# Attention logits of both heads of a pair on the two halves of the array, and a gate mask without the query's own sum

## The chip, the cores and the metric

The kernel runs on one core of one Trainium2 chip. The metric is device time in microseconds; the kernel before took 1919.86 us (median of three runs, 1917.96 to 1921.83). The core has a matrix engine (PE, with its weight loads shown apart as PEld), a vector engine (DVE), a scalar engine (ACT), a third elementwise engine (POOL) and DMA queues, which are fed by SP. Each engine runs its own instructions in a fixed order and waits on semaphores for the others.

## The reference, cut to what matters

Two transformer blocks run one after the other on 512 tokens of width 1024. The first block has two layers. Each layer has four kinds of attention with four heads each, then an output projection per kind and a feed-forward part. The second block (dilated attention, pooling, gates) is not part of the change.

```python
for l in range(2):                       # first block
    proj = rms_norm(x, norm1[l]) @ w_in[l]
    o_a = causal attention, head width 96 (latent)
    o_b = sliding window of 128 keys, with a sink logit
    o_c = causal attention over the 128 best keys of each query (indexer, top-k)
    o_d = causal attention with a forget gate:
          s = q.k/8 + (cum[t] - cum[s]);  s = where(s_pos <= t_pos, s, -inf);  softmax(s) @ v
    x = x + concat(o_a, o_b, o_c, o_d) @ w_out[l]
    x = x + square(relu(rms_norm(x, norm2[l]) @ w_up[l])) @ w_down[l]
```

In the gated attention (`o_d`) the term cum[t] of the query is the same for all its keys, so that the softmax does not depend on it.

## The kernel before, in words

All products are made from numbers split into a high and a low part, so that one product is three matmuls: high by high, high by low, low by high (`mm3`, L159 to L161 in the profile). Four blocks of 128 tokens are handled one by one.

A layer's attention part goes, in the order of the program text, through the letters of `ORDER = "LI123AZVPDCBadcb"`: latent inputs (L), indexer (I), index scores and top-k of blocks 1 to 3 (1, 2, 3), latent attention of two pairs of heads (A, Z), gated values (V) and keys (P), gated attention (D), selected attention with its own projections (C), sliding window with its own projections (B), and the four output projections (a, d, c, b). A scheduler then places the instructions of each engine. It favours what comes first in the text and moves later work into places where an engine would otherwise wait; the order is fixed when the kernel is built. The top-k rounds (L574 maximum of 8, L575 replace, L576 the mask) have a low priority and fill DVE. So projections of a later letter fill PE between the steps of an earlier attention.

Attention works on a pair of heads (`mixed_pair`). For each head, `softmax` makes four blocks of logits (one for 128 queries each, over 128 to 512 keys; for the window 128 or 256). A block is three matmuls into a PSUM bank of the tag "sc" (two banks). Then DVE adds the mask and takes the row maximum in one instruction (L335), with the sums written to a tile `p` in SBUF. ACT takes the exponentials of the head's four blocks (L345) after the maxima of all four, and scales them (L355) after the reciprocal. PE transposes the blocks of `p` (L378), ACT and DVE split the transposes into `pt`, and PE multiplies them with the values (L309, L310, L312, tile `pv`). There were two `p` tiles. The heads of C, B and D are 64 wide: the q and k of the first head of a pair lie in partitions 0 to 63 of the tile `seg`, those of the second in 64 to 127. The latent heads are 96 wide. The projections write to PSUM banks of the tag "acc" (two banks), as do the output projections; the banks are free again when ACT and DVE have read them.

For the gated attention, `forgetting` loads the negated sums of the keys for one head, spread over all partitions, into the tile `nrow` (one buffer, a DMA from DRAM), and per block DVE builds a mask from `nrow`, the query's own sum and the causal mask (L811, 128x128 to 128x512) before the block's L335.

In the second block, `pair_attention` has logits of 64-wide heads too (L1174), and there the three matmuls of both heads are written alternately in the program text.

Of the kernel before, what the change touches and what calls it, by code (L numbers as in the profile page):

```python
# [11 lines left out]
F32 = mybir.dt.float32  # L12
F32R = mybir.dt.float32r
AF = mybir.ActivationFunctionType
ALU = mybir.AluOpType
# [3 lines left out]
P = 128  # L19
S = 512  # L20
# [6 lines left out]
TAKEN = -3.0e38  # L27
EPS = 1e-6
TOPK = 128
SEGS, MIXES, PBUFS, PTS, VS = 4, 5, 2, 2, 4  # L30
QKS, V2S, PB2, B2S, GATES, PT2 = 6, 3, 2, 7, 4, 3
AHEAD, RAWS, HIS, TMPS, HALVES = 2, 2, 4, 3, 4
FIRST, KZS = 3, 2
# [24 lines left out]
class Kern:  # L58
# [43 lines left out]
        return self.tmp.tile([P, D], F32, tag="tmp", name=self.name("tmp"), bufs=TMPS)  # L102

    def half(self):
        return self.tmp.tile([P, S], F32, tag="t2", name=self.name("t2"), bufs=HALVES)

    def stat(self, cols=16):
        return self.small.tile([P, 16], F32, tag="st", name=self.name("st"), bufs=11)[:, :cols]
# [203 lines left out]
            mm(out, both, th[0], start=False, stop=True)  # L312


    def softmax(self, hd):


        nc = self.nc
        spans = hd["spans"] = hd["spans"]() if callable(hd["spans"]) else hd["spans"]
        offs, tot = [], 0  # L320
        for k0, n, _ in spans:
            offs.append(tot)
            tot += n
        pb = self.att.tile([P, 1280], F32, tag="p", name=self.name("p"), bufs=PBUFS)
        hd["p"], hd["at"] = pb, offs
        mx, sm, nm, rc = (self.astat() for _ in range(4))
        for i, (k0, n, mask) in enumerate(spans):
            sc = self.psum("sc")[:, :n]
            tok = slice(i * P, (i + 1) * P)
            self.mm3(  # L330
                sc, tuple(a[:, tok] for a in hd["q"]), tuple(a[:, k0 : k0 + n] for a in hd["k"]), True, True
            )
            if callable(mask):
                mask = mask(i, n)
            nc.vector.tensor_tensor_reduce(  # L335
                out=pb[:, offs[i] : offs[i] + n], in0=sc, in1=mask, scale=1.0, scalar=TAKEN,
                op0=ALU.add, op1=ALU.max, accum_out=mx[:, i : i + 1],
            )
        if hd.get("sink") is not None:
            nc.vector.tensor_scalar(nm, mx, hd["sink"], -1.0, ALU.max, ALU.mult)  # L340
        else:
            nc.vector.tensor_scalar(nm, mx, -hd["scale"], None, ALU.mult)
        for i, (k0, n, _) in enumerate(spans):
            s = pb[:, offs[i] : offs[i] + n]
            nc.scalar.activation(  # L345
                s, s, AF.Exp, bias=nm[:, i : i + 1], scale=hd["scale"], accum_out=sm[:, i : i + 1]
            )
        if hd.get("sink") is not None:
            es = self.astat()
            nc.scalar.activation(es, nm, AF.Exp, bias=hd["sink"])  # L350
            nc.vector.tensor_tensor(sm, sm, es, ALU.add)
        nc.vector.reciprocal(rc, sm)
        for i, (k0, n, _) in enumerate(spans):
            s = pb[:, offs[i] : offs[i] + n]
            nc.scalar.activation(s, s, AF.Copy, scale=rc[:, i : i + 1])  # L355
# [4 lines left out]
    def mixed_pair(self, heads, v, order):  # L360

        nc = self.nc
        m = self.mix()
        total = sum(len(g) for g in order)
        for x, hd in enumerate(heads):
            self.softmax(hd)
            spans = hd["spans"]
            pv = self.psum("pv")
            nmm = 0
            for group in order:  # L370
                pt = self.psum("tp")
                at, cols = 0, []
                for j in group:
                    who = [i for i, (k0, n, _) in enumerate(spans) if k0 <= j * P < k0 + n]
                    cols.append((j, at, who))
                    for i in who:
                        src = hd["at"][i] + j * P - spans[i][0]
                        nc.tensor.transpose(pt[:, at : at + P], hd["p"][:, src : src + P], self.ident)  # L378
                        at += P
                th = self.new_pt()  # L380
                self.split(th[:, 0, :at], th[:, 1, :at], pt[:, :at])
                for j, a, who in cols:
                    w = len(who) * P
# [94 lines left out]
    def consts_first(self):  # L478
        nc, c, t = self.nc, self.fc, self.t

        def load(name, shape, src):
            o = c.tile(shape, F32, tag=name, name=name)
            nc.sync.dma_start(o, src)
            return o

        self.rope64 = load("rope64", [P, NB, 128], t["c_rope64"].rearrange("(b p) c -> p b c", p=P))
        self.rope32 = load("rope32", [P, NB, 64], t["c_rope32"].rearrange("(b p) c -> p b c", p=P))
        self.causal = load("causal", [P, S], t["c_causal"])
        self.swa = load("swa", [P, 256], t["c_swa"])
        self.tri = load("tri", [P, P], t["c_tri"])  # L490
        self.full_spans = [(0, (i + 1) * P, self.causal[:, S - (i + 1) * P :]) for i in range(NB)]
        self.ones = c.tile([P, P], F32, tag="ones", name="ones")
        nc.vector.memset(self.ones, 1.0)

    def indexer(self, l, hT):

        nc = self.nc
        chunks = self.weights(3)
        kst = self.att.tile([P, S], F32R, tag="nrow", name=self.name("kst"), bufs=1)
        acc = self.att.tile([P, 256 + 384 + 512], F32, tag="dsa", name=self.name("dsa"), bufs=1)  # L500
        self.dsa = [(self.causal[:, 384:512], P)]
        offs = (None, 0, 256, 640)
# [5 lines left out]
        def rotate(b):  # L508
            pj = self.token_proj(hT, chunks, b, I_N)
            if b:  # L510
                r = self.att.tile([P, 320], F32, tag="ir", name=self.name("ir"), bufs=3)[:, :I_N]
                nc.scalar.copy(r[:, 288:296], pj[:, 288:296])
                self.idx.append(r)
            else:
                r = self.half()[:, :I_N]
            h = slice(0 if b else 8, 9)
            rv = r[:, 0:288].rearrange("p (a c) -> p a c", a=9)
            self.rope(rv[:, h], pj[:, 0:288].rearrange("p (a c) -> p a c", a=9)[:, h], self.rope32, b)
            return rv
# [212 lines left out]
    def window(self, l, hT):  # L732
        nc, t = self.nc, self.t
        sink = self.att.tile([P, 4], F32, tag="sink", name=self.name("sink"), bufs=1)
        nc.sync.dma_start(sink, t["swa_sinks"][l].partition_broadcast(P))
        sg = self.seg()
        vs = [self.new_v() for _ in range(2)]

        def values(b, src):
            for g in range(2):  # L740
                self.put_v(vs[g], b, src[:, g * 64 : g * 64 + 64].unsqueeze(1).to_broadcast([P, 2, 64]))

        self.roped(hT, self.weights(2), sg, 0)
        self.roped(hT, self.weights(2), sg, 2, values)
        spans = [(max(0, i - 1) * P, P if i == 0 else 2 * P, self.swa[:, 128:] if i == 0 else self.swa)
                 for i in range(NB)]
        return self.two_pairs(
            sg, vs, BAND, spans=spans, scale=0.125, sink=lambda h: sink[:, h : h + 1]
        )
# [47 lines left out]
    def forgetting(self):  # L797
# [2 lines left out]
        sg = self.gated_seg  # L800

        def spans(hh):
            nrow = self.att.tile([P, S], F32, tag="nrow", name=self.name("nrow"), bufs=1)
            nc.sync.dma_start(
                nrow.rearrange("p (b c) -> p b c", b=NB),
                neg.rearrange("(b h) c -> h b c", h=4)[hh].partition_broadcast(P),
            )

            def bias(i, m):
                o = self.att.tile([P, S], F32, tag="bias", name=self.name("bias"), bufs=2)[:, :m]  # L810
                nc.vector.scalar_tensor_tensor(  # L811
                    o, nrow[:, :m], cum[:, i, hh : hh + 1], self.causal[:, S - m :], ALU.add, ALU.add
                )
                return o

            return [(0, (i + 1) * P, bias) for i in range(NB)]

        return self.two_pairs(sg, vs, FULL, spans=lambda h: lambda: spans(h), scale=1.0)

    def selected(self, l, hT):  # L820
# [5 lines left out]
        for b in range(NB):  # L826
            pj = self.token_proj(hT, ch, b, 256)
            for n in range(2):
                self.put_v(vs[n], b, pj[:, n * P : (n + 1) * P].rearrange("p (h c) -> p h c", c=64))
        return self.two_pairs(sg, vs, FULL, spans=[(0, n, a) for a, n in self.dsa], scale=0.125)  # L830

    def first_tiles(self, hT, block, count):

# [262 lines left out]
    def pair_inputs(self, hp, hT):  # L1096
# [12 lines left out]
        for g, which in HEADS2:  # L1109
# [12 lines left out]
            if which < 2:  # L1122
# [1 line left out]
                self.split(nat(o[:, 0]), nat(o[:, 1]), perm(pj), 0.125 if which == 0 else None)  # L1124
                qk[g, which] = o
                continue
            vT = self.half()
            nc.scalar.copy(nat(vT), perm(pj))
            v = self.new_v()
            pt = self.psum("tq")  # L1130
# [357 lines left out]
```

## Time and profile before

| | |
|---|---|
| median of three runs | 1919.86 us |
| the profiled execution | 1920.97 us, its span 1918.9 us |
| attention of layer 0, gated heads and C's projections beside them | 137 to 200.3 us |
| C, B and the output projections of layer 0 | 200.3 to 312 us |
| the same two stretches in layer 1 | 804 to 873 us, 873 to 985 us |
| PE busy over the span | 95% |
| DVE, ACT, POOL busy over the span | 62%, 44%, 29% |

The matmul rows of the profile start at the true times, but their lengths overlap: how long one occupies PE is read from the start of one to the start of the next. DVE rows overlap a little too.

### The profile page before, as it was taken

The page shows a single profiled execution, that of the slowest core. Times are in us where ns is not written, and L with a number is a line of the kernel's source. Part 1 is how long each engine was busy: PE and PEld are TensorE (multiplying, and loading weights), DVE is VectorE, ACT ScalarE, POOL GpSimd, SP SyncE. Part 2 cuts the span into 40 slices and gives each one's busy share as a digit, 9 for nine tenths or more (in the row PEclk, how much of TensorE's full clock was granted, in tenths as well). Part 3 has the DMA queues.
Part 4 walks back from the last instruction along what each step waited for, and adds up shares of the span by engine and source line. Part 5 has one row for each costly group of instructions (what it writes and reads, how often), then busy time and mean ns, then how long its engine had stood idle before and what let it go on. Part 6 is the DMA issues. An engine that isn't in the chain of part 4 may idle for free.

```text
span 1918.9 us, 25696 instructions
## 1 busy us (share of the span) xinstructions
PE 1825.1 (95%) x9414; PEld 1524.4 (79%) x9414; DVE 1184.9 (62%) x2381; ACT 852.7 (44%) x1842; POOL 565.8 (29%) x396
## 2 busy tenths in 40 slices
PE   7899998999999998999989999999798999999898
PEld 7778877888877887888778888888776787777677
DVE  6899666555545378996774443344728644559675
ACT  5656765332323256567653233233434344534223
POOL 1334331111101113343311111111245443433454
PEclk9899999999999998999999999999899999999999
DMA  5232112444465322221133333333332332322242
GB/s 160 59 83 61 45 49 80 141 144 143 134 185 156 95 66 59 81 64 45 45 99 99 99 90 98 99 88 99 114 86 59 89 100 67 88 61 78 66 148 99
DMA packets 220651, 178.51 MB, mean 93 GB/s; under 512 B 14734, under 2 KB 191278, under 8 KB 220526
## 3 DMA queue, kind: packets, MB, share of 16 engines
q1 hardware_dynamic: 220526, 176.88, 31.3%
q8 instruction: 74, 1.21, 0.3%
q14 instruction: 51, 0.42, 0.1%
HBM read 172.50 MB, written 8.03 MB: 94 GB/s over the span
## 4 chain that ended last, share of the span: by engine, by line
PE 76%; DVE 13%; DMA 5%; ACT 2%; issue 2%; POOL 1%; SPq 0%; DVEq 0%; ACTq 0%; POOLq 0%
PE acc L159 19%; PE acc L160 18%; PE acc L161 18%; PE sc L159 5%; PE sc L160 4%; PE sc L161 4%; DMA raw<-in_w_in_dram 2%; PE tp L378 2%; PE pv L310 1%; DVE p L1235 1%; DVE b L1077 1%; PE pv L309 1%; ACT whi L142 1%; DVE dsa L554 1%; DMA raw<-in_w_down_dram 1%
## 5 line engine op out<-in xcount | busy, mean ns | idle before, releaser
L142 ACT ACTIVATE whi<-raw 128x1024 fp32r<-128x1024 f32 (+6 forms) x288 | 289.2, 1005 | 621.8 <-PE acc L160 243.5
L159 PE MATMUL acc<-hTh,whi 128*128 128x512 f32 (+1 forms) x1128 | 438.0, 389 | 11.4 <-DVE kz L167 4.7
L160 PE MATMUL acc<-hTl,whi 128*128 128x512 f32 (+1 forms) x1128 | 434.6, 386 | 0.9 <-DVE hTl L167 0.9
L161 PE MATMUL acc<-hTh,wlo 128*128 128x512 f32 (+1 forms) x1128 | 434.1, 385 | 0.0
L143 POOL TENSOR_TENSOR wlo<-raw,whi 128x1024 fp32r<-128x1024 f32 (+4 forms) x143 | 312.7, 2191 | 375.8 <-ACT whi L142 354.1
L143 DVE TENSOR_TENSOR wlo<-raw,whi 128x1024 fp32r<-128x1024 f32 (+2 forms) x145 | 177.3, 1224 | 199.4 <-ACT whi L142 199.3
L871 POOL TENSOR_TENSOR tmp<-tmp 128x512 f32<-128x512 f32 x64 | 104.8, 1639 | 609.8 <-ACT tmp L869 609.8
L159 PEld LDWEIGHTS acc<-hTh,whi 128*128 128x128 f32 x1128 | 215.1, 191 | 57.6 <-issue 7.1
L160 PEld LDWEIGHTS acc<-hTl,whi 128*128 128x128 f32 x1128 | 215.0, 191 | 41.6 <-DVE hTl L167 2.4
L161 PEld LDWEIGHTS acc<-hTh,wlo 128*128 128x128 f32 x1128 | 214.8, 190 | 40.3
L159 PE MATMUL acc<-whi,hTh 128*128 128x256 f32 (+3 forms) x512 | 156.4, 307 | 6.5 <-DVE v L167 4.3
L161 PE MATMUL acc<-whi,hTl 128*128 128x256 f32 (+3 forms) x512 | 156.4, 306 | 0.2
L160 PE MATMUL acc<-wlo,hTh 128*128 128x256 f32 (+3 forms) x512 | 153.6, 301 | 0.4 <-DVE wlo L143 0.4
L159 PEld LDWEIGHTS acc<-whi,hTh 128*128 128x128 f32 x512 | 98.9, 193 | 11.8 <-DVE v L167 4.9
L159 PE MATMUL acc<-whi,act 128*128 128x512 f32 x256 | 98.9, 392 | 3.4 <-DVE x L889 2.8
L161 PEld LDWEIGHTS acc<-whi,hTl 128*128 128x128 f32 x512 | 98.6, 193 | 3.7 <-issue 1.2
L160 PEld LDWEIGHTS acc<-wlo,hTh 128*128 128x128 f32 x512 | 99.0, 193 | 2.1 <-DVE wlo L143 0.8
L160 PE MATMUL acc<-wlo,act 128*128 128x512 f32 x256 | 100.3, 392 | 0.0
L161 PE MATMUL sc<-whi,act 128*128 128x512 f32 x256 | 99.6, 389 | 0.0
L159 PE MATMUL sc<-whi,act 128*128 128x512 f32 x256 | 99.6, 389 | 0.0
L160 PE MATMUL sc<-wlo,act 128*128 128x512 f32 x256 | 99.6, 389 | 0.0
L161 PE MATMUL acc<-whi,act 128*128 128x512 f32 x256 | 99.0, 392 | 0.1
(336 smaller groups left out, 3535.8 us busy)
## 6 DMA issues: line engine op xcount, KB each, us to landing
raw<-in_w_in_dram SPq DMA_DIRECT2D x92, 512.0 KB, 4.0
raw<-in_w_up_dram SPq DMA_DIRECT2D x64, 512.0 KB, 4.1
raw<-in_w_down_dram SPq DMA_DIRECT2D x64, 512.0 KB, 3.5
raw<-in_w_out_dram SPq DMA_DIRECT2D x24, 512.0 KB, 3.5
raw<-in_w_ada_dram SPq DMA_DIRECT2D x24, 512.0 KB, 4.0
raw<-in_w_in_dram SPq DMA_DIRECT2D x8, 416.0 KB, 5.1
x<-in_x_dram SPq DMA_DIRECT2D x4, 512.0 KB
nrow<-neg SPq DMA_DIRECT2D x8, 256.0 KB, 4.0
```

Source lines behind the costliest of these rows:

```text
L142: self.nc.scalar.activation(hi, raw, AF.Copy)
L143: self.lo_engine.tensor_tensor(lo, raw, f(hi), ALU.subtract)
L159: mm(out, lhsT[0], rhs[0], start=first, stop=False)
L160: mm(out, lhsT[0], rhs[1], start=False, stop=False)
L161: mm(out, lhsT[1], rhs[0], start=False, stop=last)
L309: mm(out, both, th[0], start=first, stop=False)
L310: mm(out[0:64], v[:, j, x, 0], th[1], start=False, stop=False)
L378: nc.tensor.transpose(pt[:, at : at + P], hd["p"][:, src : src + P], self.ident)
L554: nc.vector.scalar_tensor_tensor(a, e, r[:, 288 + h : 289 + h], self.causal[:, S - n :] if h == 0 else a, ALU.mult, ALU.add)
L871: nc.gpsimd.tensor_tensor(r[:, S:], r[:, :S], r[:, :S], ALU.mult)
L1077: nc.vector.reciprocal(dst, dst)
L1235: nc.vector.tensor_tensor(e, e, fac.to_broadcast([P, m, n]), ALU.mult)
```

## The change: what it does

For the 64-wide heads (C, B, D) a new function `logits` makes the blocks of both heads of a pair together: for each block of queries, the three matmuls of the first head and those of the second are written alternately. The first head uses partitions 0 to 63 and the second 64 to 127. Blocks 0 and 2 of the two heads take the two "sc" banks, blocks 1 and 3 the two "acc" banks. `softmax` then runs per head as before. There are three `p` tiles in place of two.

For the gated attention the mask leaves out the query's sum. `nrow` is loaded for the first three blocks of keys, and a second tile `own` for the diagonal blocks, to which the causal mask is added once per head (one DVE instruction of 128x512). A block's DVE step becomes two instructions, one over the keys before the diagonal and one over the diagonal block, with two maxima that are joined at the end. To make room in SBUF, the half tiles have 384 columns, `nrow` shares a tag with three buffers, the indexer's keys share the tag of the values, and in the second block a copy of the values uses the larger scratch tile.

```diff
-SEGS, MIXES, PBUFS, PTS, VS = 4, 5, 2, 2, 4
+SEGS, MIXES, PBUFS, PTS, VS = 4, 5, 3, 2, 4
...
+    def logits(self, heads):
...
+        for i in range(NB):
+            tok = slice(i * P, (i + 1) * P)
+            scs = []
+            for hd in heads:
+                k0, n, _ = hd["spans"][i]
+                scs.append(self.psum(("sc", "acc")[i % 2] if len(heads) > 1 else "sc")[:, :n])
+            for x, y in ((0, 0), (0, 1), (1, 0)):
+                for hd, sc in zip(heads, scs):
+                    k0, n, _ = hd["spans"][i]
+                    nc.tensor.matmul(
+                        sc, hd["q"][x][:, tok], hd["k"][y][:, k0 : k0 + n], start=x + y == 0, stop=x == 1
+                    )
+            for hd, sc in zip(heads, scs):
+                masks, mx, at = hd["spans"][i][2], hd["mx"], hd["at"][i]
+                if len(masks) > len(mx):
+                    mx.append(self.astat())
+                for m, (a, z, what) in enumerate(masks):
+                    to = mx[len(masks) - 1 - m]
+                    nc.vector.tensor_tensor_reduce(
+                        out=hd["p"][:, at + a : at + z], in0=sc[:, a:z], in1=what, scale=1.0, scalar=TAKEN,
+                        op0=ALU.add, op1=ALU.max, accum_out=to[:, i : i + 1],
+                    )
+        for hd in heads:
+            if len(hd["mx"]) > 1:
+                m0, m1 = hd["mx"]
+                nc.vector.tensor_tensor(m0[:, 1:NB], m0[:, 1:NB], m1[:, 1:NB], ALU.max)
...
+        side = heads[0]["q"][0].shape[0] == 64
+        if side:
+            self.logits(heads)
         for x, hd in enumerate(heads):
+            if not side:
+                self.logits([hd])
             self.softmax(hd)
...
-            nrow = self.att.tile([P, S], F32, tag="nrow", name=self.name("nrow"), bufs=1)
...
-                nc.vector.scalar_tensor_tensor(
-                    o, nrow[:, :m], cum[:, i, hh : hh + 1], self.causal[:, S - m :], ALU.add, ALU.add
-                )
...
+            nrow = self.att.tile([P, 384], F32, tag="ir", name=self.name("nrow"), bufs=3)
+            nc.sync.dma_start(nrow.rearrange("p (b c) -> p b c", b=NB - 1), src[0 : NB - 1].partition_broadcast(P))
+            own = self.att.tile([P, NB, P], F32, tag="bias", name=self.name("own"), bufs=2)
+            nc.sync.dma_start(own, src.partition_broadcast(P))
+            causal = self.causal[:, S - P :].unsqueeze(1).to_broadcast([P, NB, P])
+            nc.vector.tensor_tensor(own, own, causal, ALU.add)
```

How the change moves the instructions is seen in the order in which they stand on each engine. In layer 0, on PE, at the start of the gated attention, before: `sc` is a block of logits of one gated head, `acc_2136` C's first projection.

```order
L159 MATMUL sc_1804<-seg_1662 128x128
L160 MATMUL sc_1804<-seg_1663,seg_1662 128x128
L161 MATMUL sc_1804<-seg_1662,seg_1663 128x128
L161 MATMUL acc_2136<-whi_1765,hTl_111 128x256
L159 MATMUL acc_2136<-whi_1765,hTh_110 128x256
L160 MATMUL acc_2136<-wlo_1766,hTh_110 128x256
L159 MATMUL sc_1811<-seg_1662 128x256
L160 MATMUL sc_1811<-seg_1663,seg_1662 128x256
```

Now, on PE at the end of the gated attention's logits (`acc_2010` and `acc_2011` are the last blocks of heads 2 and 3, `tp` transposes of an earlier head's `p`), `acc_2136` is again C's first projection.

```order
L338 MATMUL sc_1999<-seg_1662,seg_1663 128x384
L338 MATMUL acc_2010<-seg_1662 128x512
L338 MATMUL acc_2010<-seg_1663,seg_1662 128x512
L338 MATMUL acc_2010<-seg_1662,seg_1663 128x512
L338 MATMUL acc_2011<-seg_1662 128x512
L338 MATMUL acc_2011<-seg_1663,seg_1662 128x512
L338 MATMUL acc_2011<-seg_1662,seg_1663 128x512
L310 MATMUL pv_1874<-pt_1900,v_1512 64x256
L312 MATMUL pv_1874<-pt_1900,v_1512 128x256
L406 MATMUL tp_1934<-ident,p_1809 128x128 x4
L406 MATMUL tp_1946<-ident,p_1809 128x128 x2
L159 MATMUL acc_2136<-whi_1732,hTh_110 128x256
```

C's first projection stood ahead of the first gated logits and ran between them; now it stands behind the last of the four heads' logits.

On DVE, before, the readers of C's first projection (L285 to L287, `t<-acc_2136`) and of the first gated blocks (L335) in layer 0 stand as follows.

```order
L285 TENSOR_TENSOR t_480_2161<-acc_2136,rope_98 128x256
L286 TENSOR_TENSOR t_481_2162<-acc_2136,rope_98 128x4x32
L287 TENSOR_TENSOR t_481_2162<-acc_2136,rope_98 128x4x32
L352 RECIPROCAL sa_1427<-sa_1425 128x4
L335 ISA p_1799,sa_1800<-sc_1804,bias_1808 128x128
L335 ISA sa_1800 128x1
```

Now, on DVE, the last gated block (L348, the former L335), and behind it the same reader of C's first projection.

```order
L348 ISA p_1972,sa_1995<-acc_2011,nrow_1967 128x384
L348 ISA sa_1995 128x1
L348 ISA p_1972,sa_1973<-acc_2011,own_1969 128x128
L348 ISA sa_1973 128x1
L604 MAX m_211_936<-dsa_491 128x8
L428 TENSOR_TENSOR total_1905<-pv_1874,total_1905 64x512
L167 TENSOR_TENSOR pt_1939<-tp_1934,pt_1939 128x512
L355 TENSOR_TENSOR sa_1966<-sa_1966,sa_1992 128x3
L355 TENSOR_TENSOR sa_1973<-sa_1973,sa_1995 128x3
L605 MATCH_REPLACE dsa_491<-m_211_936,dsa_491 128x512
L365 TENSOR_SCALAR sa_2025<-sa_1966 128x4
L285 TENSOR_TENSOR t_472_2161<-acc_2136,rope_98 128x256
```

All reductions of the four gated heads have moved ahead of C's first projection on DVE as well.

On PE in the selected attention of layer 0, before: `sc_2653` and `sc_2658` are logits of C's second head, `p_2567` the first head's probabilities, and `acc_2937` a projection of B.

```order
L161 MATMUL acc_2937<-whi_2444,hTl_111 128x256
L159 MATMUL sc_2653<-seg_2122 128x384
L378 MATMUL tp_2603<-ident,p_2567 128x128
L160 MATMUL sc_2653<-seg_2123,seg_2122 128x384
L161 MATMUL sc_2653<-seg_2122,seg_2123 128x384
L159 MATMUL sc_2658<-seg_2122 128x512
L378 MATMUL tp_2603<-ident,p_2567 128x128
L160 MATMUL sc_2658<-seg_2123,seg_2122 128x512
L161 MATMUL sc_2658<-seg_2122,seg_2123 128x512
L159 MATMUL acc_2937<-whi_2444,hTh_110 128x256
```

Now, on PE at the same place: `acc_2602` is the last block of C's second head, `acc_2724` and `acc_2725` belong to heads 2 and 3, and `tp<-p_2567` are the first transposes of the first head.

```order
L338 MATMUL acc_2602<-seg_2122,seg_2123 128x512
L338 MATMUL acc_2724<-seg_2122 128x256
L338 MATMUL acc_2724<-seg_2123,seg_2122 128x256
L338 MATMUL acc_2724<-seg_2122,seg_2123 128x256
L338 MATMUL acc_2725<-seg_2122 128x256
L338 MATMUL acc_2725<-seg_2123,seg_2122 128x256
L338 MATMUL acc_2725<-seg_2122,seg_2123 128x256
L406 MATMUL tp_2625<-ident,p_2567 128x128 x2
L406 MATMUL tp_2635<-ident,p_2567 128x128
L338 MATMUL sc_2734<-seg_2122 128x384
```

The projections of B that stood between the logits of C have moved behind all of them, and the three matmuls of a block mostly stand together, head after head.

## Rows read from the trace of the kernel before

**Rows 1.** The page: busy time of the engines.

```profile
PE 1825.1 (95%) x9414; PEld 1524.4 (79%) x9414; DVE 1184.9 (62%) x2381; ACT 852.7 (44%) x1842; POOL 565.8 (29%) x396
```

**Rows 2.** Windows: length, busy us of PE, PEld, DVE, ACT, POOL; PE clock.

```profile
142.50:200.30 57.80, 57.40 (x412) 50.77 (x412) 56.57 (x156) 37.46 (x95) 21.42 (x16) 1.00 0.20 57
200.30:312.00 111.70, 111.58 (x648) 91.04 (x647) 73.36 (x201) 76.55 (x190) 44.10 (x33) 1.00 0.19 59
813.00:873.00 60.00, 59.77 (x431) 53.39 (x432) 57.48 (x162) 40.49 (x100) 25.13 (x18) 1.00 0.21 58
873.00:985.00 112.00, 109.53 (x630) 88.78 (x629) 77.55 (x201) 74.20 (x187) 40.51 (x32) 1.00 0.18 57
```

**Rows 3.** Timeline, PE, second block: start, length, instruction, count.

```profile
1405.27 0.39 PE L160 MATMUL acc<-hTl,whi 128*128 128x512 f32 x1
1405.50 0.39 PE L161 MATMUL acc<-hTh,wlo 128*128 128x512 f32 x1
1405.82 0.62 PE L1174 MATMUL sc<-qk,qk 64*128 64x256 f32 x3
1406.37 0.50 PE L159 MATMUL acc<-hTh,whi 128*128 128x512 f32 x1
...
1412.07 0.62 PE L1174 MATMUL sc<-qk,qk 64*128 64x256 f32 x6
1412.62 0.50 PE L159 MATMUL acc<-hTh,whi 128*128 128x512 f32 x1
```

**Rows 4.** PE, C's projections of layer 0: two starts, then the tile's row.

```profile
148.34 0.28 PE L159 MATMUL acc<-whi,hTh 128*128 128x256 f32 x1
148.46 0.28 PE L160 MATMUL acc<-wlo,hTh 128*128 128x256 f32 x1
...
L161 PE MATMUL acc<-whi,hTl x96: 278/283/387, 137.4 to 200.8; 128*128 128x256 f32 x96
```

**Rows 5.** DVE from 142.5 to 200.3 us by shape: count, busy us, mean ns.

```profile
L574 DVE MAX8 m<-dsa 128x8 f32<-128x512 f32 x13 | 8.9, 683 | 0.0
L575 DVE MATCH_REPLACE8 dsa<-m,dsa 128x512 f32<-128x512 f32 x13 | 8.7, 672 | 0.0
L811 DVE SCALAR_TENSOR_TENSOR bias<-nrow,cum,causal 128x512 f32<-128x512 f32 x4 | 7.5, 1874 | 0.0
L167 DVE TENSOR_TENSOR pt<-tp,pt 128x512 fp32r<-128x512 f32 x10 | 6.8, 677 | 0.1
...
L335 DVE CUSTOM_DVE_ANT_0 p<-sc,bias 128x384 f32<-128x384 f32 x4 | 2.2, 540 | 0.0
L335 DVE CUSTOM_DVE_ANT_0 p<-sc,bias 128x256 f32<-128x256 f32 x4 | 1.7, 414 | 0.0
...
L335 DVE DVE_READ_ACCUMULATOR2_ANT sa<- 128x1 f32 x18 | 1.4, 79 | 0.0
...
L335 DVE CUSTOM_DVE_ANT_0 p<-sc,bias 128x128 f32<-128x128 f32 x4 | 1.0, 260 | 0.0
```

**Rows 6.** Timeline, DVE, around the gated attention of layer 0.

```profile
139.00 1.63 DVE L576 TENSOR_SCALAR dsa<-dsa 128x384 f32<-128x384 f32 x1
...
161.16 5.31 DVE L811 SCALAR_TENSOR_TENSOR bias<-nrow,cum,causal 128x384 f32<-128x384 f32 x2
...
203.37 0.68 DVE L575 MATCH_REPLACE8 dsa<-m,dsa 128x512 f32<-128x512 f32 x1
203.96 0.41 DVE L167 TENSOR_TENSOR pt<-tp,pt 128x256 fp32r<-128x256 f32 x1
...
204.49 0.41 DVE L576 TENSOR_SCALAR dsa<-dsa 128x512 f32<-128x512 f32 x1
```

**Rows 7.** Timeline, ACT: the softmax of one head of C.

```profile
219.75 0.39 ACT L345 ACTIVATE p<-p,sa 128x128 f32<-128x128 f32 x1
...
221.84 0.19 ACT L345 ACTIVATION_READ_ACCUMULATOR p<-p,sa 128x1 f32 x1
...
224.37 1.91 ACT L355 ACTIVATE p<-p,sa 128x128 f32<-128x128 f32 x4
```

More of the change, by code (lines that the diff above doesn't have):

```diff
@@ L104, in half @@
     def half(self):
-        return self.tmp.tile([P, S], F32, tag="t2", name=self.name("t2"), bufs=HALVES)
+        return self.tmp.tile([P, 384], F32, tag="t2", name=self.name("t2"), bufs=HALVES)
     def stat(self, cols=16):
@@ L312, in pv @@
             mm(out, both, th[0], start=False, stop=True)
+    def logits(self, heads):
+        nc = self.nc
+        for hd in heads:
+            spans = hd["spans"] = hd["spans"]() if callable(hd["spans"]) else hd["spans"]
+            offs, tot = [], 0
+            for k0, n, _ in spans:
+                offs.append(tot)
+                tot += n
+            hd["p"] = self.att.tile([P, 1280], F32, tag="p", name=self.name("p"), bufs=PBUFS)
+            hd["at"] = offs
+            hd["mx"] = [self.astat()]
+        for i in range(NB):
[20 more added lines that the diff above has]
+                    )
+        for hd in heads:
+            if len(hd["mx"]) > 1:
+                m0, m1 = hd["mx"]
+                nc.vector.tensor_tensor(m0[:, 1:NB], m0[:, 1:NB], m1[:, 1:NB], ALU.max)
@@ L315, in softmax @@
     def softmax(self, hd):
         nc = self.nc
[L319 to L331, printed above, removed]
-            )
[L333 to L338, printed above, removed]
+        spans, pb, offs, mx = hd["spans"], hd["p"], hd["at"], hd["mx"][0]
@@ L339, in softmax @@
+        sm, nm, rc = (self.astat() for _ in range(3))
         if hd.get("sink") is not None:
@@ L490, in consts_first @@
         self.tri = load("tri", [P, P], t["c_tri"])
-        self.full_spans = [(0, (i + 1) * P, self.causal[:, S - (i + 1) * P :]) for i in range(NB)]
+        self.full_spans = [
+            (0, (i + 1) * P, [(0, (i + 1) * P, self.causal[:, S - (i + 1) * P :])]) for i in range(NB)
+        ]
         self.ones = c.tile([P, P], F32, tag="ones", name="ones")
@@ L498, in indexer @@
         chunks = self.weights(3)
-        kst = self.att.tile([P, S], F32R, tag="nrow", name=self.name("kst"), bufs=1)
+        kst = self.att.tile([P, 2 * S], F32R, tag="v", name=self.name("kst"), bufs=self.vbufs)[:, :S]
         acc = self.att.tile([P, 256 + 384 + 512], F32, tag="dsa", name=self.name("dsa"), bufs=1)
@@ L510, in rotate @@
             if b:
-                r = self.att.tile([P, 320], F32, tag="ir", name=self.name("ir"), bufs=3)[:, :I_N]
+                r = self.att.tile([P, 384], F32, tag="ir", name=self.name("ir"), bufs=3)[:, :I_N]
                 nc.scalar.copy(r[:, 288:296], pj[:, 288:296])
@@ L744, in window @@
         self.roped(hT, self.weights(2), sg, 2, values)
-        spans = [(max(0, i - 1) * P, P if i == 0 else 2 * P, self.swa[:, 128:] if i == 0 else self.swa)
-                 for i in range(NB)]
+        spans = [(0, P, [(0, P, self.swa[:, P:])])]
+        spans += [((i - 1) * P, 2 * P, [(0, 2 * P, self.swa)]) for i in range(1, NB)]
         return self.two_pairs(
@@ L802, in spans @@
         def spans(hh):
-            nrow = self.att.tile([P, S], F32, tag="nrow", name=self.name("nrow"), bufs=1)
[L804 to L810, printed above, removed]
-                nc.vector.scalar_tensor_tensor(
-                    o, nrow[:, :m], cum[:, i, hh : hh + 1], self.causal[:, S - m :], ALU.add, ALU.add
-                )
-                return o
-            return [(0, (i + 1) * P, bias) for i in range(NB)]
+            src = neg.rearrange("(b h) c -> h b c", h=4)[hh]
+            nrow = self.att.tile([P, 384], F32, tag="ir", name=self.name("nrow"), bufs=3)
[4 more added lines that the diff above has]
+            nc.vector.tensor_tensor(own, own, causal, ALU.add)
+            out = []
+            for i in range(NB):
+                a = i * P
+                out.append((0, a + P, ([(0, a, nrow[:, :a])] if i else []) + [(a, a + P, own[:, i])]))
+            return out
         return self.two_pairs(sg, vs, FULL, spans=lambda h: lambda: spans(h), scale=1.0)
@@ L829, in selected @@
                 self.put_v(vs[n], b, pj[:, n * P : (n + 1) * P].rearrange("p (h c) -> p h c", c=64))
-        return self.two_pairs(sg, vs, FULL, spans=[(0, n, a) for a, n in self.dsa], scale=0.125)
+        return self.two_pairs(sg, vs, FULL, spans=[(0, n, [(0, n, a)]) for a, n in self.dsa], scale=0.125)
     def first_tiles(self, hT, block, count):
@@ L1126, in pair_inputs @@
                 continue
-            vT = self.half()
+            vT = self.scratch()[:, :S]
             nc.scalar.copy(nat(vT), perm(pj))
```

## The prediction

> **What bounds the kernel now.** I read the page's busy times first, then the windows of the attention stages, then single rows in them. By the page PE is the busy engine [rows 1], so a change that takes PE time away looks like a gain of its whole size. The windows say where that holds. From 200.3 to 312 us, with C, B and the output projections of layer 0, PE is busy all the time and DVE two thirds of it. From 142.5 to 200.3 us, with the gated heads D, PE and DVE are both nearly full, 57.40 and 56.57 of 57.8 us; layer 1 shows the same pair of stretches [rows 2]. The reader is to see that in the first stretch PE is full only because C's twelve projections, 96 triples of matmuls from 137.1 to 200.8 us [rows 4], stand between the steps of D. D alone is DVE work: reductions, splits, and the top-k rounds, whose last mask comes at 204.49 us [rows 6].
>
> **What the pairing removes from PE.** A lone head's block of three 256-column matmuls takes 0.55 us from its start to the next matmul's, where the pace of such matmuls elsewhere is 0.12 us, or 0.36 for three; the 512-column matmul ahead of it takes 0.32 us to the next start where its neighbour takes 0.23 [rows 3, 4]. So each uninterrupted group of 64-row matmuls pays 0.09 going in and 0.19 inside and going out, about 0.29 us beside its columns. In the second block six alternating matmuls of two heads take the same 0.55 us [rows 3]: a full pair costs what one head costs.
>
> But the order of the changed kernel alternates in only 13 of the 48 pairs of blocks; elsewhere the second head's bank comes free later and its three matmuls follow in a group of their own, often in one long run. Counted from the order, C and B of layer 0 go from 35 groups to 16 and, taking two heads' neighbouring matmuls as one step, from 95 steps to 72 (34 to 15 and 95 to 71 in layer 1). That is 19 x 0.29 = 5.5 us and 23 steps of about 0.13 us, 3.1 us: **8.6 us less PE per layer**. D's four heads save about 2.5 us in the same way, but in the first stretch, treated next.
>
> **What it moves: C's projections.** In the new order all logits of D's four heads stand ahead of C's first projection, since they hold the "acc" banks. So PE has only D's own steps there, and DVE sets the pace. From D's first reduction to the release of the first "acc" bank DVE has, by the order: 18 reductions of 128 columns, 4 of 256 and 3 of 384 (4.7 + 1.7 + 1.6 us), 25 accumulator reads (2.0), 8 rounds of top-k (5.5 + 5.4, and 0.6 for their loads at the length of a read), 6 splits of 512 columns, 3 of 256 and 2 totals at a split's length (4.1 + 1.2 + 1.4), 2 additions of the causal mask and 6 instructions on a few columns [rows 5]. The trace has no such mask addition; from below it is a 256-column reduction, 0.41, from above a 512-column L811 with its waits, 1.87 [rows 5]; I take a split's length, 0.68, since it reads and writes as much, 1.4 us for both. The small ones I put at most at a 128-column reduction, 1.6 us. Together 31 us. DVE instructions overlap: 0.68 and 0.41 of length take 0.59 to the next start and on [rows 6]; over the stretch the lengths add up to 67.1 us against 56.57 busy [rows 2]. With that 0.84, 31 become 26 us. It starts about 142.5 us: the second top-k mask starts at 139.0 us [rows 6], and what the new order puts ahead of D's first reduction beyond that is some 3.5 us. So C's first projection starts at 168.6 us instead of 137.1.
>
> Behind it PE is the bound: 288 matmuls of 256 columns at 0.118 us, 34.0; 36 transposes and 13 logits of D and C, some 5.8; 24 products with values, 3.6; about 1 us for changes of mode. That is 44.4 us, and C's projections end at 213.0 us instead of 200.8 [rows 4]: **12.1 us late per layer**. D's cheaper mask is in this sum: a head loses 4 mask builds and gains one addition, three more reductions with reads and one joining. So is the loss of stalls like the 5.31 us of two L811 [rows 6]. The DMAs of `nrow` and `own` are two per head instead of one, but for a pair they are issued before it starts, and the third buffer takes the wait for `nrow` away. I count nothing for them.
>
> **What it adds: waits in C and B.** Before, projections stood between single blocks of logits. Now the logits of a pair, and the free half of the next pair's, stand together, and behind them nothing until the first head's transposes. These wait for the softmax: exponentials from 219.75 to 222.03 us, reciprocal, then 1.91 us of scaling, 2.3 + 0.2 + 1.9 [rows 7], and 0.6 for the last reduction's own way, 5.0 us. C and B each have such a place per layer, 10 us; the other pair's first blocks, four of 256 or 128 columns per stage, cover about 2.5 us of each. **5 us uncovered per layer**; the bounds are 0, if other work slides in, and 10, if that cover has been used up by then. The third `p` tile lets only one head of the next pair go ahead: the fourth head's reductions wait for the first head's transposes, and what stands behind them on DVE waits too.
>
> [...]
>
> **The sum.** Per layer 12.1 - 8.6 + 5.0 = 8.5 us, 17 us for two. The second block keeps its order but for a few neighbours, and the feed-forward parts too. Made against the profiled execution, 1920.97 us, that is 1938; the median shown lies 1.1 us under that execution, so I predict 1937 us.
>
> **Rivals.** *PE bounds everything.* If DVE in D takes less than these rows add up to, or C's projections still fill PE, only the saved PE time counts: 2 x (8.6 + 2.5) = 22 us, 1898 us against the median. For it speaks the page's 95%; against it the order on PE, where nothing of C stands between D's logits. It decides from the point where the time from D's first reduction to C's first projection falls to some 15 us, the PE work in it. [...]
>
> *The shift and the saving cancel.* In the kernel before, the logits of C's last block wait for the top-k mask at 204.49 us [rows 6]; in the new order that mask comes before C's logits. If, besides, the waits of C and B are covered, a layer stands at 12.1 - 8.6, less the waits of the stage before, which are about 5 us of its 111.7 by my count of its matmuls: -1.5 us, -3 in all, 1917 us. For it speaks that the scheduler places later work wherever it can; against it that the "acc" banks, which that work needs, are held by logits.
>
> *More is lost.* The bursts find no cover (10 us for 5), and the mask additions and small DVE steps stall like L811 does, some 4 us per layer: 2 x (12.1 - 8.6 + 10 + 4) = 35 us, 1955 us. For it speak the 5.31 us [rows 6], against it that eight such additions replace 32 mask builds.
>
> **How the numbers follow.** The forecast 0.66, PE bounds everything 0.14, the cancelling case 0.12, more lost 0.08. The forecast's own range is 1926 to 1948, from its two bounds on the waits and 3 us either way on the shift. The whole range, 1906 to 1956, reaches toward 1898 as far as half the way of the saving and takes in the worse case. A change of 0.2%, 3.8 us, is about what a measurement can tell from none here. Faster: 0.14 and a quarter of the cancelling case, 0.17. Same: most of the rest of that case, 0.09. Slower: 0.74.
>
> **What would show it.** In the profile after: the first C projection on PE some 26 us behind D's first reduction and not beside it; PE with gaps of some 10 us in that stretch while DVE is full; the last C projection about 12 us later than before; one gap of a few us ahead of the first transposes of C and of B that ends with the scaling on ACT; and a group of six alternating logits as long as three. It would be wrong if PE stayed full from 142 to 200 us, or if the stage from C's last projection to the end of the output projections took under 103 us where it took 111.7.

## The result, and the profile after

The changed kernel takes 1970.3 us (median of 4 runs, 1966.98 to 1972.59), the kernel before 1919.16 us in runs beside it; the ratio is 1.0263, 95% interval 1.0244 to 1.0282. It is slower by 51 us where 17 were forecast, and above the whole range, which ends at 1956. The profiled execution has a span of 1967.7 us (before 1918.9).

The page, busy time of the engines and the row of the granted clock in 40 slices; it answers to [rows 1].

```profile
PE 1841.6 (94%) x9414; PEld 1539.6 (78%) x9414; DVE 1164.4 (59%) x2413; ACT 856.5 (44%) x1842; POOL 562.2 (29%) x396
...
PEclk9898889999999999978899999999899999999999
```

TensorE is busy longer than before with as many matmuls. Busy time went up as its granted clock went down, from a mean of 0.981 to 0.953: the attention of D, C and B of the two layers stands in slices 4 to 6 and 18 to 20 (of 49.2 us each), where the row falls to 8 and 7.

Windows of the changed kernel in layer 0, which answer to [rows 2]: from D's first reduction to C's first projection, C's projections, from their end to B's first projection, B's projections, from their end to the first output projection, and the output projections.

```profile
143.20:170.40 27.20, 23.98 (x87) 16.95 (x88) 25.66 (x98) 18.30 (x45) 6.24 (x4) 0.59 0.17 47
170.40:214.60 44.20, 44.19 (x355) 42.44 (x356) 30.00 (x86) 25.44 (x58) 20.55 (x16) 1.00 0.17 49
214.60:235.50 20.90, 16.62 (x64) 10.69 (x62) 8.73 (x36) 13.72 (x40) 4.70 (x2) 0.67 0.16 51
235.50:265.90 30.40, 30.40 (x253) 30.00 (x253) 16.42 (x49) 19.64 (x44) 12.49 (x14) 1.00 0.10 36
265.90:286.80 20.90, 14.49 (x74) 10.15 (x72) 9.86 (x49) 11.58 (x39) 5.34 (x4) 0.63 0.20 60
286.80:336.40 49.60, 49.60 (x240) 41.56 (x238) 30.97 (x52) 25.44 (x56) 17.23 (x10) 0.98 0.22 64
```

The reader is to see that projections and attention now take turns. In three stretches TensorE has dense work and a granted clock of 0.98 to 1.00. In the other three, the attention of D, C and B by itself, it is partly idle and has means of 0.59, 0.67 and 0.63. Shorter windows of the trace show two levels there: 1.00 from 169.1 to 220.2 us, 0.50 from 220.3 to 233.8, 1.00 from 233.9 to 271.4 and 0.50 from 271.5 to 288.4. Before, there were no such stretches: [rows 2] show 1.00 throughout.

Timeline of TensorE in the changed kernel: the start of C's projections, their end, and the stretch behind them.

```profile
169.44 0.82 PE L406 MATMUL tp<-ident,p 128*128 128x128 f32 x6
170.41 0.36 PE L159 MATMUL acc<-whi,hTh 128*128 128x256 f32 x1 [0.15 <-DVE sa L348]
...
214.88 0.28 PE L161 MATMUL acc<-whi,hTl 128*128 128x256 f32 x1
...
220.41 0.62 PE L338 MATMUL acc<-seg,seg 64*128 64x256 f32 x2
223.16 2.42 PE L406 MATMUL tp<-ident,p 128*128 128x128 f32 x8 [2.12 <-ACT p L378]
227.25 0.68 PE L338 MATMUL sc<-seg 64*128 64x384 f32 x1 [1.67 <-DVE sa L348]
...
235.47 0.39 PE L159 MATMUL acc<-whi,hTh 128*128 128x256 f32 x1
```

C's first projection is released by a reduction of D (L348), which frees the "acc" bank. Between C's last projection and B's first one there are logits, transposes and value products of C alone, and a wait ahead of the first transposes that ends with the scaling on ACT (L378). Eight transposes take 2.42 us here, at a granted clock of 0.50; below, in a stretch at 1.00, 1.09.

Timeline of DVE in the changed kernel: the first addition of the causal mask to a head's own block, and D's first reduction.

```profile
139.56 0.68 DVE L840 TENSOR_TENSOR own<-own,causal 128x512 f32<-128x512 f32 x1
...
143.21 0.26 DVE L348 CUSTOM_DVE_ANT_0 p<-sc,own 128x128 f32<-128x128 f32 x1
```

Where the time came from, by the starts of the same instructions: C's last projection in layer 0 is at 214.88 us instead of 200.8 [rows 4], 14.1 late; the end of the output projections is at 336.4 instead of 312.4, 24.0 late; the first activation of the feed-forward part is 25.9 late in layer 0 (361.9 for 336.0) and 52.9 in layer 1 (1063.2 for 1010.3). Each layer's attention loses 26 to 27 us; the end of the program is 48.8 late, so some 4 us come back in the second block.

### The profile page after: what moved, and what is told of

Read it like the earlier page. It is cut to its first block, busy times and chain, and to the rows that moved or that the text cites. A ratio compares the mean times of both kernels' runs of the same rounds, so it can differ in the third digit from the quotient of the medians.

```text
span 1967.7 us, 25751 instructions
## 1 busy us (share of the span) xinstructions
PE 1841.6 (94%) x9414; PEld 1539.6 (78%) x9414; DVE 1164.4 (59%) x2413; ACT 856.5 (44%) x1842; POOL 562.2 (29%) x396
## 4 chain that ended last, share of the span: by engine, by line
PE 74%; DVE 15%; ACT 4%; DMA 4%; issue 2%; POOL 1%; SPq 0%; ACTq 0%; DVEq 0%; POOLq 0%
PE acc L159 19%; PE acc L160 18%; PE acc L161 18%; PE sc L161 3%; PE sc L160 3%; PE sc L159 3%; DMA raw<-in_w_in_dram 2%; PE sc L338 1%; PE acc L338 1%; DVE dsa L605 1%; DVE m L604 1%; PE tp L406 1%; DVE p L1264 1%; ACT p L368 1%; DVE b L1106 1%
```

## Experiments

The theory after the result: logits that take "acc" banks keep the next stage's projections out of the attention, in C and B as in D. The rivals: the pairing itself, which makes two softmaxes late at a time; the new mask with its DMAs; and the lower clock as a cause of its own.

**The mask alone.** Every head by itself, logits in "sc":

```diff
-        side = heads[0]["q"][0].shape[0] == 64
+        side = False
```

> The new mask and the three p tiles, but each head's logits by themselves and in the sc banks, as before the change. If the loss comes from the acc banks that the logits hold: the median of before or a little less, 1905 to 1922 us, granted clock about 0.98, C's projections of layer 0 beside D and at an end near 200 us. If the loss comes from the mask or its two DMAs per head: 1945 us or more, with D's stretch longer on DVE.

Measured: 1908.76 us, ratio to before 0.9942 (0.9919 to 0.9964), clock 0.981 to 0.988. The mask isn't the cause; it is a gain of 11 us.

**Pairs, but in "sc" alone.**

```diff
-                scs.append(self.psum(("sc", "acc")[i % 2] if len(heads) > 1 else "sc")[:, :n])
+                scs.append(self.psum("sc")[:, :n])
```

> The changed kernel, but every block of logits in the two sc banks, none in acc. If the acc banks are the cause: projections stand between the logits again, the granted clock is back at 0.97 or more, and the pairing shows what it saves on PE: before less up to 2 x 11 us, 1890 to 1912 us. If the cause is that two heads' logits stand together and both softmaxes come late, whichever the banks: PE still waits in C and B, and 1945 to 1970 us.

Measured: 1919.68 us, ratio 0.9995 (0.9986 to 1.0005), between the two ranges. With the pairs kept, the banks make 50.6 us. But the expected gain isn't there: the pairs cost 11 us over the mask alone. Windows of the kernel with the mask alone, from C's first projection over the ends of C's and B's projections to the end of the output projections, and then the same of the kernel with pairs in "sc":

```profile
136.50:198.20 61.70, 60.27 (x429) 53.15 (x429) 56.06 (x187) 41.35 (x103) 24.14 (x18) 1.00 0.20 57
198.20:245.80 47.60, 47.28 (x332) 40.98 (x331) 29.37 (x89) 35.98 (x90) 20.46 (x19) 1.00 0.14 46
245.80:307.70 61.90, 60.91 (x307) 47.71 (x306) 42.87 (x101) 36.92 (x94) 22.59 (x14) 1.00 0.24 72
```

```profile
136.10:195.10 59.00, 57.09 (x413) 50.55 (x413) 53.93 (x179) 36.05 (x89) 22.84 (x17) 1.00 0.22 60
195.10:241.20 46.10, 44.98 (x319) 39.73 (x318) 25.64 (x89) 33.11 (x85) 19.62 (x18) 0.96 0.14 47
241.20:310.10 68.90, 63.53 (x336) 49.59 (x335) 45.06 (x109) 45.22 (x113) 23.92 (x15) 0.98 0.21 64
```

The busy time of TensorE falls from 168.5 to 165.6 us, with as many matmuls. But the clock column of the paired kernel is below 1.00: twice the missing share of its last two stretches, 0.96 and 0.98, is 3.7 and 2.8 us at a clock of 0.50 (an estimate from the two levels that the changed kernel's trace shows). With this time counted half, 162.4 us of work at the full clock are left. So pairing saves some 6 us of TensorE work in layer 0 (an estimate); in layer 1, counted in the same way, some 5. It is lost again: idle time rises from 2.7 to 8.4 us, and the lower clock costs some 3. In the paired kernel's timeline six alternating logits of 256 columns take 0.55 us, as three do [rows 3], and most of the idle time stands at the end of B, behind the last head's sum, where no output projection is left to fill it:

```profile
257.73 0.39 PE L338 MATMUL sc<-seg 64*128 64x256 f32 x2
257.95 0.40 PE L338 MATMUL sc<-seg,seg 64*128 64x256 f32 x4
258.28 0.50 PE L309 MATMUL pv<-pt,v 128*128 128x512 f32 x1
...
298.60 0.38 PE L309 MATMUL pv<-pt,v 128*128 128x256 f32 x1 [1.48 <-DVE total L428]
...
302.59 0.79 PE L159 MATMUL acc<-whi,mix 128*128 128x512 f32 x1 [2.84 <-ACT mix L420]
```

**No pairs, but "acc" banks.** Every head by itself, its blocks in "sc" and "acc" in turn:

```diff
-        side = heads[0]["q"][0].shape[0] == 64
+        side = False
...
-                scs.append(self.psum(("sc", "acc")[i % 2] if len(heads) > 1 else "sc")[:, :n])
+                scs.append(self.psum(("sc", "acc")[i % 2] if heads[0]["q"][0].shape[0] == 64 else "sc")[:, :n])
```

> No pairing: each head's logits by themselves, but its blocks in the sc and acc banks in turn, with the new mask. If the acc banks are the cause: as slow as the changed kernel or slower by the unsaved PE time, 1965 to 1990 us, with the clock near 0.95. If the pairing is the cause: near before, 1905 to 1930 us.

Measured: 1972.57 us, ratio 1.0266 (1.0248 to 1.0283), clock 0.95. Without a single pair the loss is whole, 63.8 us over the mask alone. Windows of this kernel from the end of C's and of B's projections to the next stage's first matmul show the same two stretches at nearly the length and clock of the changed kernel's:

```profile
217.50:238.90 21.40, 17.69 (x61) 12.12 (x61) 9.81 (x35) 15.26 (x42) 4.69 (x2) 0.58 0.16 50
270.90:292.10 21.20, 16.32 (x68) 12.04 (x66) 9.76 (x49) 13.23 (x45) 5.07 (x4) 0.61 0.19 58
```

**D alone, and C and B alone.** The changed kernel's pairs with both kinds of bank in one part, heads one by one in "sc" in the other (the first new line for D alone, the second for C and B alone):

```diff
-        side = heads[0]["q"][0].shape[0] == 64
+        side = heads[0]["q"][0].shape[0] == 64 and heads[0]["scale"] == 1.0
+        side = heads[0]["q"][0].shape[0] == 64 and heads[0]["scale"] < 1.0
```

> Pairs with sc and acc banks in the gated attention D alone; C and B head by head in sc, as before the change. By the acc banks, D's share is the later C projections, 12 to 14 us per layer less about 2.5 us of PE and what C regains: 1930 to 1948 us; the rest of the loss, 22 to 40 us, belongs to C and B. If the whole loss is D's: 1960 us or more. If D's late projections are made up for in C: 1910 to 1925 us.

> The complement of the kernel with pairs in D alone: pairs with sc and acc banks in C and B, D head by head in sc. If the costs of the stages add up, the 36 us between D alone (1934) and the changed kernel (1970) stand on top of the mask alone (1909): 1940 to 1950 us. If D's late projections make C's and B's bursts worse: below 1935 us.

Measured: D alone 1933.94 us, ratio 1.0071 (1.0056 to 1.0086); C and B alone 1940.56 us, ratio 1.0125 (1.011 to 1.014). Over the mask alone that is 25.2 and 31.8 us, 57.0 together; the changed kernel stands 61.5 above it. The costs nearly add up, and C and B have the larger one. With D alone, C's stretch up to the end of B's projections is back at the full clock, though it starts 18.6 us later than with the mask alone (216.8 for 198.2):

```profile
216.80:260.40 43.60, 43.60 (x305) 37.58 (x304) 23.44 (x83) 30.77 (x80) 17.22 (x17) 1.00 0.17 54
260.40:321.10 60.70, 59.71 (x307) 47.45 (x306) 42.77 (x99) 37.26 (x94) 23.24 (x14) 1.00 0.23 70
```

**Pairs in D and C, B by itself, all in "sc".** The search for a version that keeps the saving:

```diff
-        side = heads[0]["q"][0].shape[0] == 64
+        side = heads[0]["q"][0].shape[0] == 64 and heads[0].get("sink") is None
...
-                scs.append(self.psum(("sc", "acc")[i % 2] if len(heads) > 1 else "sc")[:, :n])
+                scs.append(self.psum("sc")[:, :n])
```

> Pairs in D and C in the sc banks, B head by head. In the kernel with all pairs in sc, D and C together were 4.7 us shorter in layer 0 than with the mask alone and as long in layer 1, while B and the output projections were 7 to 8 us longer per layer. If the pairing pays as long as projections stand beside it and costs in B, where the last softmax has nothing beside it: 1899 to 1909 us, at or a little under the mask alone. If pairs in sc cost wherever they stand: 1912 to 1920 us.

Measured: 1916.03 us, ratio 0.9999 (0.999 to 1.0008). The hope failed: pairs in "sc" cost some 8 us over the mask alone (1907.69 us, the next kernel) even where projections stand beside them. With B by itself the waits in B are shorter (1.5 us for the 2.84 above), but not the stretch, 68.7 us from the end of B's projections, with 336 matmuls in it where the mask alone leaves 307. The number of matmuls left for that end isn't by itself what costs: the next kernel, without a pair, leaves 335 there, in 66.7 us. What does cost the 8 us is not settled.

**The mask with two p tiles.**

```diff
-SEGS, MIXES, PBUFS, PTS, VS = 4, 5, 3, 2, 4
+SEGS, MIXES, PBUFS, PTS, VS = 4, 5, 2, 2, 4
...
-        side = heads[0]["q"][0].shape[0] == 64
+        side = False
```

> The mask alone (heads one by one, sc banks), with two p tiles as before the change where the mask-only kernel has three. If the mask itself makes the gain of 0.6%: 1905 to 1912 us. If the third p tile makes it: 1916 to 1922 us.

Measured: 1907.69 us, ratio 0.9946 (0.9929 to 0.9963). The gain is the mask's; the third tile gives nothing that the runs can tell from none.

**The clock, a first try.** More matmuls for TensorE, at the lowest priority:

```diff
                 pt = self.psum("tp")
+                if side and hd["scale"] < 1.0 and group is order[0]:
+                    prio = self.tc.cur_priority
+                    self.tc.cur_priority = prio + 20000
+                    for _ in range(6):
+                        nc.tensor.matmul(pt, hd["q"][0][:, :P], hd["k"][0], start=True, stop=True)
+                    self.tc.cur_priority = prio
```

> The changed kernel, and before the first transposes of each head of C and B six more matmuls of 64 rows and 512 columns into the bank that the transposes then overwrite: 48 per layer, 11 us per layer of TensorE work at 0.23 us each, at the lowest priority. Nothing else is asked of the other engines. If the granted clock is the main cost of the bursts: the clock rises over the 0.953 of the changed kernel and the time falls below 1970 us, to 1945 to 1965. If the waits for reductions and softmax are the cost: the time stays or rises by what doesn't fit in the waits, 1968 to 1990 us.

Measured: 1997.02 us, ratio 1.0411 (1.0393 to 1.0428), clock 0.952, above both ranges. It decides nothing on the clock: the scheduler put the extra matmuls where TensorE had work, for instance six at a granted clock of 0.50 between transposes (0.49 us each where 0.23 were reckoned), and the kernel became 27 us longer:

```profile
233.84 2.93 PE L404 MATMUL tp<-seg 64*128 64x512 f32 x6
```

**The clock, in the wait itself.** The same idea with an operand, the pair's maxima, that is ready only when the wait begins; four matmuls, and eight in the other kernel:

```diff
                 pt = self.psum("tp")
+                if hd.get("fill") and x == 0 and group is order[0]:
+                    for _ in range(4):
+                        nc.tensor.matmul(pt[:NB], hd["mx"][0], self.causal, start=True, stop=True)
...
+            heads[0]["fill"] = n == 0 and kw["scale"] < 1.0
             out.append(self.mixed_pair(heads, vs[n], order))
```

> The changed kernel, with four more matmuls (4 rows out, 512 columns of the causal mask in f32, result overwritten) at the first pair of C and of B, which need that pair's maxima and so start where TensorE began its longest wait; 8 per layer. [...]

> The same with eight such matmuls at each of the places, 16 per layer, longer than the wait itself. [...]

Measured: 1961.70 us with four, ratio to before 1.0231 (1.0214 to 1.0248), and 1963.67 with eight, 1.0237 (1.0221 to 1.0253). More work made the kernel 8.6 and 6.6 us faster by the medians, 6 and 5 by the ratios to before. Were the clock the main cost, I expected 1946 to 1960 us with four, and with eight less than the changed kernel's 1970; were the waits, 1968 to 1985 us with four, and with eight another 8 to 20. With four the time lies just above the range for the clock, with eight it is under 1970 us, as the clock would have it. Of the kernel with eight, the stretch between C's and B's projections and the one from B's to the output projections, and in the first the extra matmuls (each shows as two) and the transposes behind them:

```profile
215.80:234.70 18.90, 18.20 (x80) 9.05 (x78) 8.56 (x36) 12.15 (x33) 4.70 (x2) 1.00 0.16 56
265.10:287.20 22.10, 19.56 (x87) 8.96 (x85) 8.87 (x45) 11.16 (x36) 5.35 (x4) 0.77 0.17 57
```

```profile
216.07 0.28 PE L161 MATMUL acc<-whi,hTl 128*128 128x256 f32 x1
...
220.51 7.03 PE L402 MATMUL tp<-causal,sa 128*4 128x512 f32 x16
...
228.02 1.09 PE L409 MATMUL tp<-ident,p 128*128 128x128 f32 x8
```

All of the first stretch runs at a granted clock of 1.00, where the changed kernel has a mean of 0.67. Its transposes start 11.95 us after C's last projection, 3.7 later than without the fill (8.28), and still it is 2.0 us shorter (18.9 for 20.9). So the clock costs this stretch between 2.0 and 5.7 us (an estimate); the upper figure also holds the wait of 1.67 us for a reduction at 227.25 above, which the later start covers, and a few instructions that changed places. The rest of the length is mostly the chain of reductions and softmax on DVE and ACT: the scaling of a head, for one, takes ACT 1.92 us in the changed kernel, from 222.70 us at a TensorE clock of 0.50, and 1.91 before, at 1.00 [rows 2, 7]. Of the changed kernel's stretch some 13.8 us are at 0.50 (an estimate, by the 0.67 of its window), and in nearly 4 of these TensorE is idle. In B's stretch of the same kernel (the second line above) the fill doesn't hold the clock: 22.1 us at 0.77, where the changed kernel has 20.9 at 0.63.

## Why the prediction was wrong

**C's projections late, +12.1 us: right in what happens, 2 us too small in layer 0 and 6 in layer 1.** The first one was to come at 168.6, 26 us behind D's first reduction; it came at 170.41, 27.2 us behind 143.21, with DVE busy for 25.66 of 27.20 us. The projections were to take 44.4 us; they took 44.2. The late end is 14.1 us in layer 0. In layer 1 it is 18.0: C's projections end 43.9 us later there (913.0 for 869.1), of which layer 0 passed on 25.9. The mask addition, for which I took 0.68 us from a neighbour, took 0.68. TensorE has less idle time in that stretch than the forecast 10 us, 3.2, because it runs at a clock of 0.50 for some 22 of the 27.2 us (an estimate, by the 0.59 of the window).

**Less TensorE work in C and B, -8.6 us (and some 2.5 in D): right in size, mostly not by the pairing.** Each execution's span can be split by the trace: the time in which TensorE is idle; its busy time, with time at a granted clock of 0.50 counted half (the work at the full clock); and what the lower clock added. The program's matmuls are 9414 in each, without the fills:

| us | work at the full clock | idle | added by the lower clock | span |
|---|---|---|---|---|
| before | 1797.1 | 93.8 | 28.0 | 1918.9 |
| changed | 1771.2 | 126.0 | 70.4 | 1967.7 |
| no pairs, "acc" banks | 1774.2 | 116.9 | 79.6 | 1970.7 |
| pairs in "sc" | 1781.7 | 104.0 | 30.6 | 1916.3 |
| mask alone | 1794.7 | 92.9 | 15.7 | 1903.2 |
| changed, eight fills | 1798.7 | 111.8 | 47.6 | 1958.1 |

The first and the third column are estimates: the 256-column projections start 0.21 us apart at a clock of 0.50 (the changed kernel, 935.36 to 937.49 us) and 0.12 at 1.00 (from 171 us), less than twice, so that the third column is some tenth too large, and the first too small by as many us. The work falls by 25.9 us, where 2 x (8.6 + 2.5) = 22 were forecast. But without a single pair it falls by 22.9: most of the saving comes with the banks, which make the logits stand together. The uninterrupted groups of 64-row logits on TensorE are 98 before, 50 in the changed kernel and 48 in the one without pairs; at the prediction's 0.29 us a group, 50 groups fewer are 14 of the 22.9 us (an estimate). In the "sc" banks, with projections still in between (75 groups), the pairs save 12.9 us against the mask alone. That the size came out is in part luck: the prediction counted the fewer groups, and put them down to the pairing.

**Uncovered waits in C and B, +5.0 us: the step that failed.** The prediction saw that nothing stands behind the logits of a pair until the first transposes, and counted one softmax chain of 5.0 us per stage, half of it covered. That wait came as reckoned: 2.1 us in C and 2.2 in B. What failed is that it was priced as the only one, and that all other work there was priced at the full clock. TensorE's waits from the end of C's projections to B's first one, and from the end of B's projections to the first output projection (us in total, times, the longest):

```profile
PE tp L406 <- ACT p L378: 2.1, 1, 2.1
PE sc L338 <- DVE sa L348: 2.0, 2, 1.7
```

```profile
PE sc L338 <- DVE sa L348: 2.4, 2, 1.9
PE tp L406 <- ACT p L378: 2.2, 1, 2.2
PE acc L338 <- ACT seg L166: 0.9, 2, 0.5
```

The rest are waits of logits, most of them for reductions (L348), which the prediction names for the fourth head and gives no price. The windows show 4.3 idle us in C's stretch and 6.4 in B's, 10.7 where 5.0 were forecast. The second part had no term at all: by the clock column some 31 us from the end of C's projections to the end of the output projections are at a clock of 0.50 (an estimate, twice the missing share of 20.9, 20.9 and 49.6 us: 13.8, 15.5 and 2.0). If the 10.7 idle us lie in these, the lower clock adds another 10.3 us (an estimate). So where -8.6 + 5.0 = -3.6 was forecast, the stage became 9.9 us longer (from C's last projection to the end of the output projections, 111.6 us before and 121.5 after). Over the whole execution idle time rises by 32.2 us and the loss by the lower clock by 42.4.

The reason lies one step earlier. I followed the "acc" banks in D, where they push C's projections behind D's last logits. In C and B the same rule pushes B's projections behind all logits of C, and the output projections behind all of B's. I had seen the first of these in the order, and took from it one wait per stage; but the projections were the cover of every wait there, and what kept TensorE dense. The kernel without pairs but with "acc" banks shows that these banks are enough for the whole loss, and the one with pairs in "sc" that without them all but 11 of the 61.5 us over the mask alone are gone. And I read the clock's 1.00 in [rows 2] as given. It went together with the mixing of projections and attention. The two kernels with a fill in the wait show that a higher clock gives back some of the loss, 5 to 9 us net; by the table the eight fills take 22.8 us off the loss by the lower clock, and add 13.3 us of work beyond the idle time that they fill. What a full clock alone would give back is not settled: some of the time saved would become waits.

**D's cheaper mask, counted inside the first step.** By itself it is worth 10 to 12 us. In the changed kernel it is inside the 27.2 us, as reckoned.

**The rivals.** "PE bounds everything" took the saving for the gain; with all pairs in "sc" TensorE's work falls by some 6 us per layer and not 11, and idle time and the clock take more than that back. "The shift and the saving cancel" needed covered waits, and they are not covered. "More is lost", 1955 us, had the right direction and the 10 us of waits, but its other term, stalled mask additions, isn't there: all eight take 0.67 to 0.70 us. The resource that decided is PSUM: 50.6 us hang on which banks the pairs' logits get. The kernel without a pair loses as much, so it is the banks and not the pairing. The prediction drew a cost of the banks in D alone.

## What to carry to other kernels

Before work takes a second kind of PSUM bank, list who else draws on that kind, in every stage: a bank lent to logits that wait for DVE is a bank that the projections, which filled those waits, do not get. The clock column in the profile before is no constant: it fell here from 1.00 to means of 0.58 to 0.67 in the stretches where the change opened waits on TensorE, and the work around such waits has to be priced at the lower clock too. And a change of two parts is worth splitting: here one half gains 0.6% by itself, and the other half loses 3%.

## What the runs showed of the hardware

That added work can shorten a kernel: 16 more matmuls in f32 (four in each of four waits) took 8.6 us off by the medians. The transposes behind them in layer 0 ran in 1.09 and 0.98 us instead of 2.42 and 1.94, and the granted clock of the four stretches was 0.80 and 0.80 in layer 0 and 0.82 and 0.82 in layer 1, where the changed kernel has 0.67, 0.63, 0.58 and 0.64.

That pairs on the two halves of the array cost no more than one head was expected and seen, 0.55 us for six as for three [rows 3]. That this is worth only some 6 us of TensorE work per layer, with the pairs side by side as the banks allow, and that it was lost again in waits and at the lower clock, was not.
